# A two-layer trunk on one core: the second input unit's first chunk in float32, and the order of the head around it

## The chip, the cores and the metric

One core of one Trainium2 chip runs the whole kernel as one program. The metric is the device time of one execution, in microseconds (us), median of three runs. Its engines are TensorE (PE, with its weight loads, PEld), VectorE (DVE), ScalarE (ACT), GpSimd (POOL) and the queue of SyncE (SP), which issues nearly all DMAs.

## The reference

```python
def reference(x, norm_g, ...):
    for i in range(DEPTH):                 # DEPTH = 2: layer A, then layer B
        h = rmsnorm(x, norm_g[i])          # x * rsqrt(mean(x*x) + eps) * g
        if i % N_MIXERS == 0:
            x = x + recurrent_mixer(h, a_w_in, a_conv_w, ..., a_w_out)
        else:
            x = x + shortconv_mixer(h, b_w_in, b_conv_w, b_w_out)
    return rmsnorm(x, final_g)

def recurrent_mixer(h, w_in, conv_w, conv_b, gate_w, gate_b, lam, w_out):
    u = einsum('bsd,dc->bsc', h, w_in)     # 1024 -> 3072 columns
    gate, xb = u[..., :WIDTH], u[..., WIDTH:]
    xb = causal_depthwise_conv(xb, conv_w, conv_b)
    y = rg_lru(xb, gate_w, gate_b, lam)    # per head: two products, tanh/exp/sqrt, a scan
    return einsum('bsc,cd->bsd', y * silu(gate), w_out)
```

x is (1, 2048, 1024) in float32, WIDTH is 1536 in 12 heads of 128.

## The kernel before

The sequence is cut into 4 chunks of 512 columns; chunks 0 and 1 are half 0, chunks 2 and 3 are half 1. The 1024 inputs of a product are 8 blocks of 128 (`d`, or `kh` and `k`). A unit is 256 output columns of an input matrix: two heads' values (unit 0: `xb`) or two heads' gates (unit 1), so that layer A has 12 units. Float32 accuracy comes from three float16 products: every operand is split into a high and a low half, and `mm3` (lines 487 to 492) issues high x high, high x low and low x high, each 128x512, for one block.

Before a product of this kind, each block of x needs its norm (`normed`, L285, VectorE: x times gain times `inv`), its high half (`add`, L291, ScalarE) and its low half (L293, VectorE). The weights are scaled by a power of two found from their squares (`unit_squares` L363, `unit_scale` L372 to L381) and split (`split`, L399 on ScalarE, L401 on VectorE). `inv`, one value per column of x, is made from sums of squares by `inv_from`: a square root on ScalarE (L245), a reciprocal (L246) and four small diagonals (L256) on VectorE, four products of TensorE that spread the values over the partitions (`pn`, L259), and a copy out of PSUM (L262). For chunk 0 the squares are summed from x as it comes (L226, L227, and products `ss`, L233); for chunks 1 to 3 from rows of x, `xn`, on ScalarE (`sum_rows`, L1429).

Layer A's first two units go through `unit_of_blocks`, 16 `mm3` for a chunk, two PSUM accumulators at a time out of six (`acc_tile`). Only unit 0's chunk 0 is done otherwise: `first_weights` multiplies the weights by the norm's gain (L434, 16 pieces of 128x128), `first_blocks` takes the product with x as it comes, in float32 (L613, 16 products of 128x512), and `first_done` multiplies by `inv` afterwards (L625). The order on TensorE is: unit 0 chunk 0 in float32; unit 1 chunks 0 and 1; unit 0 chunk 1; units 1 and 0 on chunks 2 and 3; then units 2 and on. Between these products stand the `pn` of each chunk and, from the generator `mixer`, two float32 gate products for each of the two heads and each chunk (L907). `second` is a generator that is advanced twice at every stopping point of a unit; it makes the norms and blocks of chunks 1, 2 and 3. A planner orders each engine's instructions from the order of the program, priorities (`high_priority`), and extra edges (`after(a, b)`: a stands behind b); each engine then runs its instructions in that order.

Of the kernel before, what the change touches and what calls it, by code (L numbers as in the profile page):

```python
# [14 lines left out]
P = 128  # L15
# [31 lines left out]
def trunk(ctx, tc, xT, xn, prm, wa, ga, oa, wb, ob, out):  # L47
# [192 lines left out]

    def inv_from(ss, inv, queue, copy, behind=None):

        n = inv.shape[1] // P
        r = cst.tile([P, 4], F32, tag="r", name="r", bufs=2)[:, 0:n]
        s.activation(r, ss, AF.Sqrt, bias=epst[:, 0:1], scale=1.0 / D)  # L245
# [49 lines left out]
    def build_blocks(l, x, inv, ops):  # L295

        ins = []
        for c in range(2):  # L300
            for kh in range(2):
                for k in range(4):
                    n = normed(l, x[k + 4 * kh, c], k + 4 * kh, inv[c])
                    if len(ins) > 1:
                        after(n, ins[-2][1])
                    ins.append(add(ops, f"B{kh + 1}{c + 1}", k, x[k + 4 * kh, c]))
                yield ins[-1]
# [89 lines left out]
    def split(src, sw, behind=()):  # L397
        t = pair16(wp, "wc", "wc", 8)
        ins = [s.activation(t[:, 0, :], src, AF.Copy, scale=sw[:, 2:3])]  # L399
        ins.append(  # L400
            v.scalar_tensor_tensor(  # L401
                out=t[:, 1, :], in0=src, scalar=sw[:, 2:3], in1=t[:, 0, :],
                op0=ALU.mult, op1=ALU.subtract,
            )
        )
        for i, first in zip(ins, behind):
            after(i, first)
        return t

    def block_weights(l, wdram, w):  # L410


        raw = load_weights(wdram)
        yield
        sums = unit_squares(raw)
        yield
        sw = unit_scale(l, *sums, w["behind"])
        w["undo"] = sw[:, 3:4]
        for n in (0, 2, 1, 3):
            w[("A11", "A12", "A21", "A22")[n]] = split(raw[n], sw)  # L420
            yield

    def first_weights(wdram, w):


        raw, gained = ([sgt("w0") for n in range(4)] for i in range(2))
# [14 lines left out]
        sw = unit_scale(0, *sums, w["behind"])  # L441
# [51 lines left out]

    throttle, pe_last, blocks_last, evac_last = [None, None], [None], [None], [None]
# [81 lines left out]
    def unit_of_blocks(w, ops, dest, done, end, chunks=range(2), evict=None, pin=False):  # L576


        for c in chunks:
            accs = [acc_tile("acc") for m in range(2)]  # L580
            for kh in range(2):
                for k in range(4):
                    for m in range(2):
                        kk = slice(k * P, (k + 1) * P)
                        t, x = w[f"A{m + 1}{kh + 1}"], ops[f"B{kh + 1}{c + 1}", k]
                        blocks_last[0] = mm3(
                            accs[m], t[:, 0, kk], t[:, 1, kk], x[:, 0, :], x[:, 1, :],
                            kh + k == 0, kh + k == 4,
                        )
                        if pin:  # L590
                            pe_last[0] = blocks_last[0]
# [13 lines left out]
    def first_blocks(w, x):  # L605


        accs = w["accs"] = [acc_tile("acc") for m in range(2)]
        behind = None
        for d in range(KB):  # L610
            kk = slice((d % 4) * P, (d % 4 + 1) * P)
            for m in range(2):
                ins = nc.tensor.matmul(  # L613
                    accs[m], w["raw"][2 * m + d // 4][:, kk], x[d, 0],
# [4 lines left out]
            behind = yield ins  # L619

    def first_done(accs, inv, behind):
        t = [xct("xb") for m in range(2)]
        for m in range(2):
            after(
                v.tensor_tensor(out=t[m][:, 3 : 3 + CH], in0=accs[m], in1=inv, op=ALU.mult),  # L625
                behind,
            )
        return t
# [26 lines left out]
    def in_proj(l, units, ops, first, side):  # L655
# [170 lines left out]
    def in_A(ops, first, head, side, before_end, beside):  # L826
# [6 lines left out]
        def pair(hp):  # L833
# [5 lines left out]
            def conv(m, half, c, a, undo=None):  # L839
# [20 lines left out]
                with tc.high_priority(1000 if undo is not None else 1):  # L860
# [105 lines left out]

            units.append((wa[2 * hp], xdest, nothing, beside, xafter, conv))
            units.append((wa[2 * hp + 1], nothing, nothing, beside, nothing, silu))
# [404 lines left out]
    prep0 = first_weights(wa[0], w0)  # L1373
    gains()
    constants()
    x0, x1, xrows = {}, {}, {}

    def load_x(x, c):
        for d in range(KB):
# [11 lines left out]
    for kh in range(2):  # L1391
        next(prep0)
        for d in range(4 * kh, 4 * kh + 4):
            x0[d, 0] = load("A", d, 0, xt("xs"))
    prep = block_weights(0, wa[1], w1)
    next(prep)
# [5 lines left out]
    blocks0 = build_blocks(0, x0, inv0, hA[0])  # L1402
# [3 lines left out]
    w0["squares"] = sq[1], sq[2], sq[3], sq[7]  # L1406
    next(prep0)
    next(prep)

    firsts = first_blocks(w0, x0)  # L1410
    for d in range(5):
        mm = next(firsts)
    w0["behind"] = mm
    ss = ps.tile([P, 4], F32, tag="g", name="ss", bufs=2)
    with tc.high_priority(PR):
        mm = sums_of(acc, ss, mm)
    next(prep0)
    mm = w1["behind"] = firsts.send(mm)
    with tc.high_priority(PR):
        mm = inv_from(ss, inv0[0], None, v.tensor_copy, mm)  # L1420
    run(prep)
    firsts.send(mm)
    blocks_last[0] = next(firsts)
    split0 = [next(blocks0) for i in range(2)]

    def sum_rows(c, behind):
        for i, t in enumerate(xrows[c]):
            after(
                s.activation(t, t, AF.Square, accum_out=rows[c % 2][:, i : i + 1]), behind  # L1429
            )  # L1430

    def inv_of_rows(c, inv):
        with tc.high_priority(PR):
            inv_from(rows[c % 2], inv, None, v.tensor_copy, blocks_last[0])


    sum_rows(1, split0[0][0])

    def head():

        return first_done(w0["accs"], inv0[0], split0[-1][1])

    def second():
        inv_of_rows(1, inv0[1])
        split0.extend(blocks0)
        w0["split"] = split0[1][0], split0[3][1]
        run(prep0)
        yield
        h = build_blocks(0, x1, inv1, hA[1])
        for c in range(2):  # L1450
            sum_rows(2 + c, split0[2 + c][0])
            for _ in range(4 - 2 * c):
                yield
            inv_of_rows(2 + c, inv1[c])
            yield
            for _ in range(2):
                next(h)
                yield
# [7 lines left out]
    first = w0, (w1, prep)  # L1466
# [289 lines left out]
```

## Time and profile before

| | |
|---|---|
| median of 3 runs | 1963.3 us (1962.35 to 1965.16) |
| the profiled execution | 1963.37 us |
| its span in the profile | 1961.6 us |
| TensorE busy | 1927.5 us, 98% of the span |
| VectorE, ScalarE, GpSimd busy | 1267.1, 1101.7, 710.6 us |

The 1.8 us between span and execution lie outside the traced instructions. Times in the rows are microseconds from the span's start unless a column says ns. A float32 product appears as two MATMUL records, a float16 product as one.

### The profile page before, as it was taken

What the parts mean: (1) busy time and instruction counts of PE and PEld (TensorE: products, weight loads), DVE (VectorE), ACT (ScalarE), POOL (GpSimd) and SP (SyncE); (2) the same over time, 40 slices, a digit from 0 to 9 for tenths busy, and PEclk for the clock granted to TensorE, in tenths of its full rate; (3) what the DMA queues carried; (4) which work ended last, traced back from release to release, by engine and by line L of the source; (5) the groups of instructions that cost most, each with busy time, mean ns of one, the idle gap of its engine ahead of it and who ended that gap; (6) DMA issues with size and microseconds to landing.
All of it is one profiled execution on the core that took longest, in us unless ns stands there. A gap on an engine that the chain in (4) does not pass through costs nothing.

```text
span 1961.6 us, 25479 instructions
## 1 busy us (share of the span) xinstructions
PE 1927.5 (98%) x8922; PEld 900.1 (46%) x8922; DVE 1267.1 (65%) x2103; ACT 1101.7 (56%) x1970; POOL 710.6 (36%) x554
## 2 busy tenths in 40 slices
PE   7899999999999999999999999999999999999998
PEld 3344444444444444444444444444444444444446
DVE  7878667777777687999435437547547436544565
ACT  6959877777767663455454553553553543544442
POOL 0012313343413030335453454564664643622321
PEclk9999999999999999999999999999999999999999
DMA  9223323332315985411041131242232220496572
GB/s 339 71 76 107 124 71 107 103 124 86 108 43 206 377 329 168 159 61 43 33 156 54 61 128 59 77 154 70 91 129 65 81 97 28 148 368 230 111 228 87
DMA packets 158289, 252.97 MB, mean 129 GB/s; under 512 B 15312, under 2 KB 58960, under 8 KB 158160
## 3 DMA queue, kind: packets, MB, share of 16 engines
q1 hardware_dynamic: 157936, 250.82, 38.2%
q8 instruction: 70, 1.15, 0.2%
q0 software_dynamic: 224, 0.53, 0.1%
q14 instruction: 59, 0.48, 0.1%
HBM read 173.16 MB, written 78.12 MB: 128 GB/s over the span
## 4 chain that ended last, share of the span: by engine, by line
PE 81%; DVE 7%; ACT 5%; issue 4%; DMA 3%; POOL 1%; SPq 0%; DVEq 0%; POOLq 0%; ACTq 0%
PE acc L488 12%; PE acc L491 12%; PE acc L492 12%; PE p L492 8%; PE p L488 8%; PE p L491 8%; PE r L488 4%; PE r L492 4%; PE r L491 4%; PE pg L907 2%; PE q L492 2%; PE q L491 2%; PE q L488 2%; DMA xs<-in_xT 1%; DVE op L293 1%
## 5 line engine op out<-in xcount | busy, mean ns | idle before, releaser
L488 PEld LDWEIGHTS <-wc 128*128 128x128 f16 x2096 | 208.0, 99 | 266.0 <-issue 30.8
L491 PEld LDWEIGHTS <-wc 128*128 128x128 f16 x2096 | 205.7, 98 | 258.4 <-issue 24.6
L492 PEld LDWEIGHTS <-wc 128*128 128x128 f16 x2096 | 205.6, 98 | 256.6 <-issue 13.5
L488 PE MATMUL acc<-op,wc 128*128 128x512 f16 x752 | 281.2, 382 | 12.5 <-ACT op L291 11.3
L492 PE MATMUL p<-op,wc 128*128 128x512 f16 x768 | 291.1, 379 | 1.1 <-DVE wc L401 1.1
L491 PE MATMUL p<-op,wc 128*128 128x512 f16 x768 | 291.1, 379 | 0.0
L488 PE MATMUL p<-op,wc 128*128 128x512 f16 x768 | 290.6, 379 | 0.1
L491 PE MATMUL acc<-op,wc 128*128 128x512 f16 x752 | 286.9, 383 | 0.7 <-DVE op L293 0.3
L492 PE MATMUL acc<-op,wc 128*128 128x512 f16 x752 | 286.5, 382 | 0.0
L932 POOL TENSOR_TENSOR u<-fixed,u 128x512 f32<-128x512 f32 x48 | 51.3, 1091 | 366.4 <-ACT fixed L929 344.8
L227 POOL TENSOR_TENSOR sa<-sa,sq 128x512 f32<-128x512 f32 x48 | 71.5, 1490 | 270.3 <-ACT sq L226 254.4
L401 DVE SCALAR_TENSOR_TENSOR wc<-wr,fixed,wc 128x512 f16<-128x512 f32 x122 | 115.0, 960 | 78.2 <-ACT wc L399 68.6
L1312 DVE SCALAR_TENSOR_TENSOR xo<-acc,fixed,xo 128x512 f32<-128x512 f32 (+1 forms) x120 | 84.8, 710 | 104.3 <-PE acc L492 100.3
L401 DVE SCALAR_TENSOR_TENSOR wc<-ws,fixed,wc 128x512 f16<-128x512 f32 x104 | 100.1, 970 | 76.6 <-ACT wc L399 76.6
L492 PE MATMUL r<-op,wc 128*128 128x512 f16 x384 | 145.5, 379 | 0.0
L491 PE MATMUL r<-op,wc 128*128 128x512 f16 x384 | 145.5, 379 | 0.0
L488 PE MATMUL r<-op,wc 128*128 128x512 f16 x384 | 145.5, 379 | 0.0
L998 POOL TENSOR_TENSOR pb<-pb,cg 128x512 f32<-128x512 f32 x48 | 67.7, 1410 | 196.0 <-DVE fixed L375 117.3
L399 ACT ACTIVATE wc<-wr,fixed 128x512 f16<-128x512 f32 x122 | 83.8, 712 | 75.5 <-DVE fixed L378 72.6
L865 DVE SCALAR_TENSOR_TENSOR u<-acc,fixed,u 128x511 f32<-128x511 f32 (+2 forms) x138 | 101.1, 741 | 31.2 <-ACT u L861 31.0
L933 DVE TENSOR_TENSOR_SCAN u<-a,fixed,u 128x512 f32<-128x512 f32 x48 | 80.5, 1681 | 38.8 <-POOL u L932 38.8
L527 ACT ACTIVATE ed<-p,fixed 128x512 f32<-128x512 f32 x72 | 49.3, 685 | 91.1 <-PE p L492 86.0
(205 smaller groups left out, 3937.4 us busy)
## 6 DMA issues: line engine op xcount, KB each, us to landing
wr<-in_wb SPq DMA_DIRECT2D x104, 256.0 KB, 3.3
zAT<-u SPq DMA_DIRECT2D x48, 256.0 KB, 2.0
zr<-zAT SPq DMA_DIRECT2D x48, 256.0 KB, 5.2
zr<-zBT SPq DMA_DIRECT2D x48, 256.0 KB, 5.2
wr<-in_wa SPq DMA_DIRECT2D x44, 256.0 KB, 3.8
zAB<-sg SPq DMA_DIRECT2D x36, 256.0 KB, 2.1
zr<-zAB SPq DMA_DIRECT2D x36, 256.0 KB, 5.4
zBB<-ed SPq DMA_DIRECT2D x36, 256.0 KB, 2.0
```

What stands on the lines that cost most here:

```text
L227: squared[0] = eng.tensor_tensor(out=acc, in0=acc, in1=sq, op=ALU.add)
L399: ins = [s.activation(t[:, 0, :], src, AF.Copy, scale=sw[:, 2:3])]
L401: v.scalar_tensor_tensor(out=t[:, 1, :], in0=src, scalar=sw[:, 2:3], in1=t[:, 0, :], op0=ALU.mult, op1=ALU.subtract,)
L488: ins = nc.tensor.matmul(acc, wh, xh, start=start, stop=False, **kw)
L491: nc.tensor.matmul(acc, wh, xl, start=False, stop=False, **kw)
L492: return nc.tensor.matmul(acc, wl, xh, start=False, stop=stop, **kw)
L527: marked["ACT"] = s.activation(d[m, c], acc, AF.Copy, scale=undo)
L865: v.scalar_tensor_tensor(out=u[:, n:], in0=a[:, 0 : CH - n], scalar=ac(3 - n), in1=u[:, n:], op0=ALU.mult, op1=ALU.add,)
L932: marked["POOL"] = g.tensor_tensor(out=u, in0=w, in1=u, op=ALU.mult)
L933: v.tensor_tensor_scan(out=u, data0=a, data1=u, initial=stA[:, h : h + 1], op0=ALU.mult, op1=ALU.add,)
L998: g.tensor_tensor(out=t, in0=t, in1=cg[m, half, c], op=ALU.mult)
L1312: ins = v.scalar_tensor_tensor(out=x[:, ts], in0=acc[:, ts], scalar=zsc[half][:, 2:3], in1=x[:, ts], op0=ALU.mult, op1=ALU.add,)
```

## The change

Unit 1's chunk 0 is taken in float32 from x as it comes too, in the way of unit 0's. Its four weight tiles are loaded between the first blocks of x, its gained copies made by 16 more pieces of L434, and its 16 products alternate with unit 0's. The norm of chunk 0 is made behind step 7 of these 16 steps and that of chunk 1 behind step 9 (each step is two products). `first_done` now takes four accumulators out, the second pair scaled by `unscale` as well, behind the last block of chunk 1; the gate function of chunk 0 then works from these copies (`gdest`). Only three of chunk 0's eight blocks are made early; the other five come behind chunk 3's. `constants` comes behind these three. Both units' weights are split behind the square root of chunk 1's norm. The copies of `inv` for chunks 1 to 3 move from VectorE to ScalarE. The convolution of unit 0's chunk 1 loses its high priority, and `norm_last` puts a chunk's first float16 product behind the `pn` of a norm.

```diff
-def first_blocks(w, x):
-    accs = w["accs"] = [acc_tile("acc") for m in range(2)]
+def first_blocks(ws, x):
+    for w in ws:
+        w["accs"] = [acc_tile("acc") for m in range(2)]
     behind = None
-    for d in range(KB):
+    for u, d in [(u, d) for u in range(2) for d in range(2)] + [
+        (u, d) for d in range(2, KB) for u in range(2)
+    ]:
+        w = ws[u]
...
-            behind = yield ins
+            behind = (yield ins) or ins
...
 def start_blocks(w0, w1):
-    take(1, 0, w1, iter(()), True, end=nothing)
-    for m in range(2):
-        units[0][1](m, 0, 0)
+    take(1, 0, w1, iter(()), True, (1,), end=nothing)
+    for u in range(2):
+        for m in range(2):
+            units[u][1](m, 0, 0)
     take(0, 0, w0, iter(()), True, (1,))
...
-                with tc.high_priority(1000 if undo is not None else 1):
+                with tc.high_priority(1 if (hp, half, c) < (0, 0, 2) else 1000):
...
+next(prep0); gains(); load_x(x0, 0, (0, 1)); next(prep1); load_x(x0, 0, (2, 3))
+next(prep0); next(prep1); load_x(x0, 0, range(4, KB))
...
+for step in range(2 * KB):
+    mm = firsts.send(mm)
+    if step == 5:
+        w0["behind"] = w1["behind"] = mm
+        ss = ps.tile([P, 4], F32, tag="g", name="ss", bufs=2)
+        with tc.high_priority(PR):
+            mm = sums_of(acc, ss, mm)
+        next(prep1)
+        next(prep0)
+    elif step == 7:
+        with tc.high_priority(PR):
+            mm = inv_from(ss, inv0[0], None, v.tensor_copy, mm)
+        sum_rows(1, rooted * 4)
+    elif step == 9:
+        mm = inv_of_rows(1, inv0[1], mm)
+        w0["split"] = w1["split"] = rooted[0]
+        run(prep1)
+        run(prep0)
+    else:
+        mm = None
+blocks_last[0] = norm_last[0] = mm
+blocks0 = build_blocks(0, x0, 0, inv0[0], hA[0])
+for _ in range(3):
+    next(blocks0)
+constants()
+chunk1 = list(build_blocks(0, x0, 1, inv0[1], hA[0]))
+sum_rows(2, [hi for hi, _ in chunk1[0::2]])
 
 def head():
-    return first_done(w0["accs"], inv0[0], split0[-1][1])
+    return first_done((w0, w1), inv0[0], chunk1[-1][1])
 
 def second():
...
+    h = [build_blocks(0, x1, c, inv1[c], hA[1]) for c in range(2)]
+    norm_last[0] = inv_of_rows(2, inv1[0], blocks_last[0])
+    yield
+    chunk2 = list(h[0])
+    sum_rows(3, [hi for hi, _ in chunk2[0::2]])
+    for _ in range(7):
         yield
+    norm_last[0] = inv_of_rows(3, inv1[1], blocks_last[0])
+    yield
+    run(h[1])
+    yield
+    run(blocks0)
+    yield
```

## Rows read from the trace of the kernel before

**Rows 1.** The page: TensorE's busy tenths in 40 slices of 49 us.

```profile
PE   7899999999999999999999999999999999999998
```

**Rows 2.** Busy time of each engine in stretches: the stretch, its length, busy us (instructions) of PE, PEld, DVE, ACT and POOL, granted clock, share of DMA engines, GB/s.

```profile
0.00:7.00 7.00, 1.01 (x4) 0.93 (x4) 2.98 (x28) 2.15 (x8) 0.31 (x5) 1.00 0.66 182
7.00:26.00 19.00, 18.67 (x52) 9.27 (x53) 14.88 (x63) 13.68 (x30) 0.00 (x0) 1.00 1.03 385
26.00:45.00 19.00, 13.62 (x57) 6.12 (x57) 15.00 (x28) 14.78 (x26) 0.00 (x0) 0.91 1.00 354
45.00:70.00 25.00, 24.31 (x112) 11.74 (x112) 20.46 (x42) 20.53 (x36) 0.00 (x0) 0.93 0.57 193
70.00:90.00 20.00, 17.17 (x60) 7.08 (x60) 19.53 (x39) 19.81 (x33) 0.00 (x0) 1.00 0.00 0
90.00:108.00 18.00, 13.51 (x50) 5.39 (x49) 12.14 (x25) 12.86 (x19) 4.25 (x4) 0.81 0.08 30
108.00:128.00 20.00, 20.00 (x94) 9.06 (x93) 19.80 (x33) 8.72 (x18) 6.67 (x5) 1.00 0.28 92
128.00:1952.00 1824.00, 1817.52 (x8488) 849.16 (x8486) 1159.27 (x1845) 1008.47 (x1803) 697.99 (x539) 1.00 0.38 126
```

**Rows 3.** What TensorE waited for from 7 to 128 us: us in total, times, the longest.

```profile
PE acc L488 <- ACT op L291: 11.3, 6, 3.5
PE pg L907 <- DVE u L874: 1.5, 2, 1.3
```

**Rows 4.** The columns of rows 2 in stretches of 2 us, around the places where the granted clock falls.

```profile
28.00:30.00 2.00, 1.76 (x6) 0.69 (x6) 1.97 (x5) 1.21 (x3) 0.00 (x0) 0.77 1.03 370
30.00:32.00 2.00, 2.00 (x7) 0.63 (x5) 2.00 (x5) 1.37 (x3) 0.00 (x0) 0.50 0.96 339
32.00:34.00 2.00, 2.00 (x10) 0.90 (x9) 1.24 (x2) 2.00 (x5) 0.00 (x0) 0.87 0.89 238
...
46.00:48.00 2.00, 2.00 (x6) 0.71 (x5) 2.00 (x4) 0.93 (x2) 0.00 (x0) 0.54 0.98 371
48.00:50.00 2.00, 2.00 (x7) 0.80 (x6) 2.00 (x4) 2.00 (x4) 0.00 (x0) 0.61 0.37 152
...
94.00:96.00 2.00, 0.97 (x3) 0.25 (x2) 2.00 (x5) 2.00 (x5) 0.00 (x0) 0.50 0.00 0
96.00:98.00 2.00, 2.00 (x6) 0.73 (x5) 2.00 (x4) 0.81 (x2) 0.00 (x0) 0.50 0.00 0
98.00:100.00 2.00, 2.00 (x6) 0.63 (x5) 2.00 (x6) 0.80 (x3) 0.00 (x0) 0.50 0.35 131
100.00:102.00 2.00, 2.00 (x9) 0.89 (x8) 2.00 (x6) 0.09 (x1) 0.00 (x0) 0.81 0.00 0
```

**Rows 5.** TensorE in order of time: start, us, line, output and inputs, number of records [idle before, and what ended it]. The row at 59.38 is the 23rd product after the one at 54.41.

```profile
7.06 11.29 PE L613 MATMUL acc<-xs,w 128*128 128x512 f32 x20 [1.45 <-DVE fixed L171]
...
22.13 3.60 PE L613 MATMUL acc<-xs,w 128*128 128x512 f32 x8
28.11 0.59 PE L488 MATMUL acc<-op,wc 128*128 128x512 f16 x2 [2.38 <-ACT op L291]
...
44.96 1.02 PE L488 MATMUL acc<-op,wc 128*128 128x512 f16 x4 [2.33 <-ACT op L291]
...
54.41 0.38 PE L491 MATMUL acc<-op,wc 128*128 128x512 f16 x1
...
59.38 0.38 PE L488 MATMUL acc<-op,wc 128*128 128x512 f16 x1
...
70.75 0.59 PE L488 MATMUL acc<-op,wc 128*128 128x512 f16 x2 [1.44 <-ACT op L291]
...
93.61 0.72 PE L488 MATMUL acc<-op,wc 128*128 128x512 f16 x2 [3.46 <-ACT op L291]
95.36 1.44 PE L488 MATMUL acc<-op,wc 128*128 128x512 f16 x3 [1.03 <-ACT op L291]
```

**Rows 6.** Groups of instructions from 7 to 128 us: line, engine, output and inputs, shapes, count | busy us, mean ns of one | idle before.

```profile
L285 DVE SCALAR_TENSOR_TENSOR xs<-xs,fixed,inv 128x512 f32<-128x512 f32 x32 | 23.6, 744 | 0.1
L293 DVE TENSOR_TENSOR op<-xs,op 128x512 f16<-128x512 f32 x32 | 21.8, 682 | 4.4 <-ACT op L291 4.4
L1429 ACT ACTIVATE xn<-xn 128x1024 f32<-128x1024 f32 x12 | 12.5, 1041 | 0.0
L613 PEld LDWEIGHTS acc<-xs,w 128*128 128x128 f32 x32 | 6.8, 221 | 9.3 <-issue 7.3 <-DVE fixed L171 1.5 <-DMA wr<-in_wa 0.2
L262 DVE COPY inv<-pn 128x512 f32<-128x512 f32 x4 | 2.7, 684 | 1.1 <-PE pn L259 1.1
```

**Rows 7.** VectorE and ScalarE in order of time, columns as in rows 5.

```profile
10.75 0.87 DVE L434 TENSOR_SCALAR w<-w,fixed 128x128 f32<-128x128 f32 x4
13.91 0.63 ACT L226 ACTIVATE sq<-xs 128x512 f32<-128x512 f32 x1 [0.17 <-DVE sa L227]
19.68 0.87 DVE L256 TENSOR_SCALAR dg<-fixed,r 128x128 f32<-128x128 f32 x4
23.27 2.74 DVE L401 SCALAR_TENSOR_TENSOR wc<-wr,fixed,wc 128x512 f16<-128x512 f32 x4 [0.67 <-ACT wc L399]
60.25 1.28 DVE L625 TENSOR_TENSOR xb<-acc,inv 128x512 f32<-128x512 f32 x2
```

**Rows 8.** SyncE's queue: the issue of the rows of chunk 1, columns as in rows 5.

```profile
11.63 2.33 SPq L1389 DMA_DIRECT2D xn<-in_xn  x4
```

More of the change, by code (lines that the diff above doesn't have):

```diff
@@ L293, in add, with build_blocks @@
         return hi, v.tensor_tensor(out=t[:, 1, :], in0=src, in1=t[:, 0, :], op=ALU.subtract)
[L295 to L307, printed above, removed]
+    built = []
+    def build_blocks(l, x, c, inv, ops):
+        for d in range(KB):
+            n = normed(l, x[d, c], d, inv)
+            if len(built) > 1:
+                after(n, built[-2][1])
+            built.append(add(ops, f"B{d // 4 + 1}{c + 1}", d % 4, x[d, c]))
+            yield built[-1]
     def build_h(l, x, inv, ks, ops, ready=()):
@@ L395, in load_weights, with split, first_weights @@
         return raw
-    def split(src, sw, behind=()):
+    def split(src, sw, behind=None):
         t = pair16(wp, "wc", "wc", 8)
[L399 to L404, printed above, removed]
-        )
-        for i, first in zip(ins, behind):
-            after(i, first)
-        return t
[L410 to L426, printed above, removed]
+        ins = s.activation(t[:, 0, :], src, AF.Copy, scale=sw[:, 2:3])
+        if behind is not None:
+            after(ins, behind)
+        v.scalar_tensor_tensor(
+            out=t[:, 1, :], in0=src, scalar=sw[:, 2:3], in1=t[:, 0, :],
+            op0=ALU.mult, op1=ALU.subtract,
+        )
+        return t
+    def first_weights(wdram, w, raw, gained):
         w["raw"] = gained
@@ L618, in first_blocks, with first_done @@
                     after(ins, behind)
-            behind = yield ins
-    def first_done(accs, inv, behind):
-        t = [xct("xb") for m in range(2)]
+            behind = (yield ins) or ins
+    def first_done(ws, inv, behind):
+        t = [xct("xb") for n in range(4)]
+        unscale = ws[1]["scale"][:, 0:1]
+        two_over(unscale, ws[1]["undo"])
+        v.tensor_scalar(
+            out=unscale, in0=unscale, scalar1=0.5, scalar2=None, op0=ALU.mult
+        )
         for m in range(2):
-            after(
-                v.tensor_tensor(out=t[m][:, 3 : 3 + CH], in0=accs[m], in1=inv, op=ALU.mult),
-                behind,
-            )
+            ins = v.tensor_tensor(
+                out=t[m][:, 3 : 3 + CH], in0=ws[0]["accs"][m], in1=inv, op=ALU.mult
+            )
+            after(ins, behind)
+        for m in range(2):
+            ins = v.scalar_tensor_tensor(
+                out=t[2 + m][:, 3 : 3 + CH], in0=ws[1]["accs"][m], scalar=unscale,
+                in1=inv, op0=ALU.mult, op1=ALU.mult,
+            )
+            after(ins, behind)
         return t
@@ L965, in silu, with gdest @@
                 gate(m, half, c)
+            def gdest(m, half, c):
+                silu(m, half, c, heads0[2 + m][:, 3 : 3 + CH], first[1][0]["undo"])
             units.append((wa[2 * hp], xdest, nothing, beside, xafter, conv))
-            units.append((wa[2 * hp + 1], nothing, nothing, beside, nothing, silu))
+            units.append((wa[2 * hp + 1], gdest, nothing, beside, nothing, silu))
         for hp in range(NH // 2):
@@ L1372, in trunk, with load_x @@
     inv0, inv1 = [[xt("inv") for c in range(2)] for half in range(2)]
-    prep0 = first_weights(wa[0], w0)
-    gains()
-    constants()
+    prep0 = first_weights(wa[0], w0, *([sgt("w0") for n in range(4)] for i in range(2)))
+    prep1 = first_weights(
+        wa[1], w1, [wrt("wr") for n in range(4)], [buf(wk, "mx", "w1", 10) for n in range(4)]
+    )
     x0, x1, xrows = {}, {}, {}
-    def load_x(x, c):
-        for d in range(KB):
+    def load_x(x, c, blocks=range(KB)):
+        for d in blocks:
             x[d, c % 2] = load("A", d, c, xt("xs"))
@@ L1389, in load_rows @@
             sp.dma_start(t, xn[r0 : r0 + P, :])
[L1391 to L1396, printed above, removed]
+    next(prep0)
+    gains()
+    load_x(x0, 0, (0, 1))
+    next(prep1)
+    load_x(x0, 0, (2, 3))
+    next(prep0)
+    next(prep1)
+    load_x(x0, 0, range(4, KB))
     load_rows(1)
@@ L1401, in trunk @@
         load_x(x1, c)
-    blocks0 = build_blocks(0, x0, inv0, hA[0])
     acc = et("sa")
     sq = [add_square(acc, x0[d, 0], d == 0, v) for d in range(KB)]
-    w0["squares"] = sq[1], sq[2], sq[3], sq[7]
+    w0["squares"] = sq[1], sq[1], sq[3], sq[3]
+    w1["squares"] = sq[1], sq[3], sq[7], sq[7]
     next(prep0)
[L1408 to L1424, printed above, removed]
+    next(prep1)
     def sum_rows(c, behind):
         for i, t in enumerate(xrows[c]):
-            after(
-                s.activation(t, t, AF.Square, accum_out=rows[c % 2][:, i : i + 1]), behind
-            )
@@ L1432, in inv_of_rows @@
-    def inv_of_rows(c, inv):
+            ins = s.activation(t, t, AF.Square, accum_out=rows[c % 2][:, i : i + 1])
+            after(ins, behind[i])
+    def inv_of_rows(c, inv, behind):
         with tc.high_priority(PR):
-            inv_from(rows[c % 2], inv, None, v.tensor_copy, blocks_last[0])
-    sum_rows(1, split0[0][0])
+            return inv_from(rows[c % 2], inv, None, s.copy, behind)
+    firsts = first_blocks((w0, w1), x0)
+    mm = None
[6 more added lines that the diff above has]
+                mm = sums_of(acc, ss, mm)
+            next(prep1)
+            next(prep0)
+        elif step == 7:
[8 more added lines that the diff above has]
+        else:
+            mm = None
@@ L1464, in ahead @@
         return w, prep
-    first = w0, (w1, prep)
+    first = w0, (w1, iter(()))
     sideA = [second()]
```

24 lines of the change are left out of this document (7 added, 17 removed).

## The prediction, made before the changed kernel ran

> **What bounds the kernel now.** I read the page's 40 slices first [rows 1]: TensorE is at nine tenths or more nearly everywhere; the first slices fall short. The stretches [rows 2] put a size on it. From 108 us on TensorE is full (20.00 of 20, then 1817.52 of 1824), so that a microsecond which the head gives back to TensorE shifts the rest of the kernel by one. From 7 to 108 us it is not full. The waits [rows 3] say why: 11.3 us in six waits for ScalarE's high halves of blocks of x, and 1.5 us of gate products behind the convolution. Then the clock: after the three longest of these waits (2.38, 2.33, 3.46 us, the last followed by 1.03) [rows 5] the granted clock falls to its lower level, 1.2 GHz, and the float16 products take twice as long [rows 4]. Busy time by (1 - clock) over these rows is 1.66 us at 28 to 34, 1.70 at 46 to 50 and 2.87 at 94 to 102: 6.2 us. So the head loses 11.3 + 1.5 + 6.2 = 19.0 us to late operands, and this is the most that a change of the head's order can earn.
>
> The operands are late because VectorE and ScalarE are nearly full themselves: 40.0 of 45 us and 40.3 of 45 from 45 to 90 [rows 2]. A block costs VectorE 0.74 + 0.68 less some overlap, about 1.36 us [rows 6], while TensorE uses one up in six products, 1.3 us: (59.38 - 54.41)/23 = 0.216 us each [rows 5].
>
> **What the change costs.** One chunk of unit 1 (16 x 3 x 0.216 = 10.4 us of float16) becomes 16 float32 products. Eight records, four products, took 3.60 us less the last one's drain, 0.43 a record [rows 5], so 0.86 a product and 13.7 us: **3.3 us more work on TensorE**. The `ss`, `pt` and `pn` products stay the same in number: nothing.
>
> Here one rule speaks against the change. The float32 weight loads take 0.22 us on average [rows 6], and the records still follow at 0.43, so the loads lie under the products before them. The Trainium skill, "TensorE: Matmul & The Clock Gate", section "Weight-path perf modes", says that fast weight load is off for float32. Were the 32 added loads bare, they would cost 32 x 0.22 = 7.0 us more; the trace shows them covered, and I add nothing.
>
> **What it removes.** Before, float16 work began at 28.11 behind a wait of 2.38 us, because chunk 0's blocks need the norm, the copy and the splits first, all after `ss`. Now TensorE has its own work meanwhile. Its float32 phase: start at 7.06, 32 products of 0.86 = 27.5; the slow beginning, where 20 records took 11.29 us instead of 8.6, so 2.7 lost, paid in both kernels; `ss`, `pt` and `pn`, which fill 18.35 to 22.13 beside two products, 2.1; one more `pn`, about 1 [rows 5]. It ends near 40. In that time VectorE and ScalarE must finish this, in order:
>
> - Chunk 0's squares. Four weight tiles (1.05 MB) now go ahead of x's last four blocks in SyncE's queue; at 385 GB/s [rows 2] these land 2.7 us later, the last square starts at 16.6 instead of 13.91 [rows 7], the sum is ready near 18. `ss` stands behind step 5, near 20: covered by 2 us.
> - The gains: 16 pieces, 0.87 for four [rows 7], 3.5 us on VectorE before 15, where it is idle 4.1 of 19 us [rows 2]; half a microsecond of wait at worst.
> - Chunk 1's norm: rows asked for at 11.63 as before, since the bytes ahead are the same [rows 8]; four squares of 1.04 + 0.1 on ScalarE [rows 6] behind a square root near 21, another root, the reciprocal and 0.87 us of diagonals [rows 7]: ready near 27. Its `pn` stands behind step 9, near 29. All later float32 products are queued behind it on TensorE; the cover is 2 us, and beyond that each microsecond costs one.
> - Splits of eight weight tiles, 2.74 us for four on VectorE [rows 7], 5.5 in all, three blocks of chunk 0, 4.1, then chunk 1's. From 25.5 on this gives the first block of chunk 1 near 37 to 38.5, with TensorE there at 40. The cover is thin; if `constants` or the gains spill over it is gone. I keep half of what the same place costs now, (2.38 + 1.66)/2 = **2.0 us**.
>
> Chunk 1's eight blocks then run ahead of TensorE, and so do chunk 2's: unit 1 chunk 1 and unit 0 chunk 1 fill TensorE from 40 to about 62, while VectorE owes 8 + 8 blocks, four copies out of PSUM (0.64 each [rows 7]), and two gate functions: 22 + 2.6 + 2.6 = 27 us from 35. So the waits at 44.96 and 70 go, with the first's slow stretch. Five blocks of chunk 0 (5 x 1.36 = 6.8 us) are no longer in their way.
>
> Chunk 3 is where it is late next. Its norm is only asked for at the middle of unit 1's chunk 2, near 67, and the blocks compete with two convolutions. Before, that place cost 3.46 + 1.03 idle and 2.87 of clock, 7.4 us. With 6.8 us less ahead of them but TensorE here some 10 us earlier, I take half, **3.7 us**. The small waits between gate products stay as they are, 1.5 and the short ones, **1.9 us** in all. The copies of three `inv` go from VectorE (0.68 each [rows 6]) to ScalarE, and are taken at nothing: ScalarE's share from 90 to 128 is 21.6 of 38 [rows 2], and if that cover fails they cost 0.7 each. The five late blocks are needed only by unit 2, after 108, and cost nothing while TensorE has units 0 and 1's half 1 to do; without it, 6.8 us.
>
> The clock is the second rule that I weigh. The rows show that stalls of 2.3 us and more are followed by a stretch at 0.50, and one of 1.44 at 70 is not: the clock stays at 1.00 behind it [rows 2, 5]. The Trainium skill, same page, section "What's actually happening", calls the half rate the default that activity lifts. By it each long stall avoided earns its slow stretch too, which is what the sum already does.
>
> **Sum.** 19.0 recoverable, less 3.3, less what stays (2.0 + 3.7 + 1.9 = 7.6): 8.1 us gained. The profiled execution took 1963.4 us, its span 1961.6 and 1.8 around it; it stands 0.1 above the median. 1963.3 - 8.1 = **1955.2 us**.
>
> **The rivals.**
>
> 1. *Nearly all waits go.* If chunk 3 is covered too (TensorE can take unit 0's chunk 2 meanwhile, as the planner may order it), only 2 to 3 us stay: 19.0 - 3.3 - 2.5 = 13.2, 1950. For it: the other unit's products are there to fill in. Against: VectorE. Chance 0.14.
> 2. *VectorE becomes the bound of the head.* Its busy time up to 128 us is 104.8 [rows 2]; gains 3.5 and two more copies 1.3 come, 2.0 of `inv` copies go: 107.6. At its share of 45 to 90 us, 40.0/45 = 0.89, the work after 7 us lasts (107.6 - 3.0)/0.89 = 117.5 us, to 124.5 instead of 128: 3.5 us gained, 1959.8. Against: scans and gate functions can wait, TensorE doesn't need them by then. Chance 0.18.
> 3. *The second norm is late on TensorE.* 4 us late at `pn`, with a slow stretch of 1.7, would leave 2.4: 1960.9. Chance 0.06.
> 4. *Bare weight loads*, as worked out: 8.1 - 7.0 = 1.1 gained, 1962.2. Chance 0.02.
> 5. *Slower: the accumulators.* Four of six are now held from the first products until chunk 1's last block, and unit 1's chunk 1 takes the other two. Unit 0's chunk 1 cannot start before two are copied out. If VectorE takes chunk 2's eight blocks (10.9 us) ahead of these copies, TensorE stands about 11 us near 51, and starts again at 0.50 for the 2.9 us that such a stall cost before. 14 us on top of the 7.6: 19.0 - 3.3 - 21.6 = -5.9, 1969. It decides from a wait of about 5 us, with its clock. For it: the blocks come first in the program. Against: chunk 2's norm needs squares behind chunk 1's blocks, then two engines and `pn`, which leaves VectorE some 3 us free just then. Chance 0.12.
>
> **The numbers.** The forecast itself has 0.48, with 1951.5 to 1958.5 of its own (the terms that stay between 4 and 11 us). About 0.2%, 4 us, is what a measurement here tells from no change. Faster by more: the forecast, rival 1 and half of rival 2, with a little of 3: 0.72. Within: the rest of 2, 3 and 4: 0.16. Slower: rival 5, 0.12. The low end is the ceiling with nothing left of the waits, 1963.3 - 15.7 = 1947.6, rounded to 1947; the high end takes in rivals 2 to 4 and leaves the slower case out: 1963.
>
> **What would show it.** Right: 64 records of L613, ending near 40, with no gap over a microsecond; the float16 stream beginning within 2 us of it; granted clock 1.00 from 28 to 70; one falling stretch at most, at chunk 3's start. Wrong: TensorE waiting for `pn` near 29; a wait of several microseconds near 51 for a copy by VectorE (L625's successor); a wait for L291 and half clock at two places again; or VectorE at 19 of 20 from 45 on with TensorE below it. The prediction is wrong also if TensorE after 128 us is no longer full.

## The result, and the profile after

The changed kernel takes 1952.2 us (median of 4 runs, 1950.99 to 1953.28) against 1964.2 of the kernel before in the same comparison (1962.35 to 1966.74): a ratio of 0.9938, 95% interval 0.9926 to 0.9949, so 12.0 us faster. The profiled execution took 1953.3 us, its span 1951.5, which is 10.1 us less than the profiled execution before.

The stretches of the changed kernel (columns as in [rows 2]):

```profile
7.00:26.00 19.00, 17.61 (x49) 8.53 (x49) 16.12 (x87) 14.49 (x33) 0.00 (x0) 1.00 1.02 372
26.00:41.00 15.00, 15.00 (x47) 7.47 (x46) 14.89 (x32) 8.95 (x17) 0.00 (x0) 1.00 1.01 353
41.00:62.00 21.00, 14.51 (x57) 6.93 (x56) 18.73 (x36) 13.79 (x26) 0.00 (x0) 0.76 0.65 249
62.00:73.00 11.00, 11.00 (x52) 5.00 (x51) 9.08 (x18) 10.94 (x19) 0.00 (x0) 1.00 0.32 96
73.00:90.00 17.00, 17.00 (x80) 8.27 (x79) 15.44 (x32) 12.98 (x25) 0.00 (x0) 1.00 0.06 17
90.00:108.00 18.00, 18.00 (x76) 8.20 (x74) 15.25 (x25) 15.94 (x24) 2.13 (x2) 1.00 0.03 11
108.00:128.00 20.00, 20.00 (x90) 9.23 (x89) 15.63 (x35) 14.00 (x26) 3.59 (x3) 1.00 0.34 109
```

TensorE is full from 26 to 41 us and from 62 us on. One stretch, 41 to 62, holds nearly the whole loss. What it waited for from 7 to 128 us, where [rows 3] had six waits for ScalarE:

```profile
PE pn L261 <- DVE dg L258: 6.5, 1, 6.5
PE ss L233 <- DVE sa L227: 0.9, 1, 0.9
PE acc L605 <- DVE fixed L114: 0.5, 1, 0.5
```

The six waits for high halves are gone, and so are the gate products' waits. In their place is one wait of 6.5 us. TensorE in order of time (columns as in [rows 5]; L605 are the float32 products, L261 the products that spread a norm):

```profile
7.71 12.20 PE L605 MATMUL acc<-xs,w 128*128 128x512 f32 x24 [0.49 <-DVE fixed L114]
20.82 1.05 PE L233 MATMUL ss<-fixed,sa 128*128 128x1 f32 x8 [0.90 <-DVE sa L227]
...
30.02 1.05 PE L261 MATMUL pn<-dg,fixed 128*128 128x128 f32 x8
30.91 10.46 PE L605 MATMUL acc<-xs,w 128*128 128x512 f32 x24
...
53.05 2.07 PE L261 MATMUL pn<-dg,fixed 128*128 128x128 f32 x8 [6.49 <-DVE dg L258]
77.57 1.05 PE L261 MATMUL pn<-dg,fixed 128*128 128x128 f32 x8
```

The float32 phase runs through to 41.4 and float16 work follows without a gap. At 46.6, in the middle of unit 1's chunk 1, stand the four products of chunk 2's norm, and everything behind them waits until 53.05. They themselves then run at half speed: eight records in 2.07 us, where the same eight at 77.57 take 1.05. What they wait for, on VectorE and ScalarE:

```profile
41.54 1.06 ACT L1424 ACTIVATE xn<-xn 128x1024 f32<-128x1024 f32 x1 [2.03 <-DMA xn<-in_xn]
47.70 1.04 ACT L1424 ACTIVATE xn<-xn 128x1024 f32<-128x1024 f32 x1
49.26 0.28 ACT L247 ACTIVATE r<-fixed 128x4 f32<-128x4 f32 x1
50.00 1.28 DVE L622 TENSOR_TENSOR xb<-acc,inv 128x512 f32<-128x512 f32 x2
51.20 0.17 DVE L248 RECIPROCAL r<-r 128x4 f32<-128x4 f32 x1
51.28 1.38 DVE L627 SCALAR_TENSOR_TENSOR xb<-acc,fixed,inv 128x512 f32<-128x512 f32 x2
52.71 0.87 DVE L258 TENSOR_SCALAR dg<-fixed,r 128x128 f32<-128x128 f32 x4
```

The rows of chunk 2 land late, their squares are tied to chunk 1's blocks on ScalarE, the last begins at 47.7, and the diagonals (L258) stand behind the four copies out of PSUM on VectorE.

One more reading tells the head from what comes behind it. A small product for a weight scale (`pt`) stands behind the same work in both kernels: 32 float32 and 408 float16 records before, 64 and 360 here, and 24 records of gate products in both. It is called the mark below. Its start before (L372) and here (L374):

```profile
148.93 0.28 PE L372 MATMUL pt<-fixed 128*128 128x4 f32 x2
140.79 0.28 PE L374 MATMUL pt<-fixed 128*128 128x4 f32 x2
```

TensorE is 8.1 us ahead there. The other 2.0 of the 10.1 us come later.

### The profile page after: what moved, and what is told of

Same layout as the page of the kernel before. It is cut to its first block, busy times and chain, and to the rows that moved or that the text cites. A ratio compares the mean times of both kernels' runs of the same rounds, so it can differ in the third digit from the quotient of the medians.

```text
span 1951.5 us, 25464 instructions
## 1 busy us (share of the span) xinstructions
PE 1926.0 (99%) x8906; PEld 901.2 (46%) x8906; DVE 1267.5 (65%) x2120; ACT 1101.9 (56%) x1971; POOL 708.2 (36%) x554
## 4 chain that ended last, share of the span: by engine, by line
PE 89%; DVE 5%; DMA 3%; ACT 2%; issue 1%; POOL 0%; SPq 0%; DVEq 0%; ACTq 0%; POOLq 0%
PE acc L475 14%; PE acc L478 14%; PE acc L479 14%; PE p L479 8%; PE p L478 8%; PE p L475 8%; PE r L475 4%; PE r L479 4%; PE r L478 4%; PE pg L912 3%; PE q L479 2%; PE q L478 2%; PE q L475 2%; DVE op L295 1%; DMA xs<-in_xT 1%
## 5 line engine op out<-in xcount | busy, mean ns | idle before, releaser
L479 PE MATMUL acc<-op,wc 128*128 128x512 f16 x736 | 279.7, 380 | 0.0
L478 PE MATMUL acc<-op,wc 128*128 128x512 f16 x736 | 279.7, 380 | 0.0
L475 PE MATMUL acc<-op,wc 128*128 128x512 f16 x736 | 278.3, 380 | 0.6 <-DVE sg L966 0.3
```

Of the source, the lines that this page charges most:

```text
L475: ins = nc.tensor.matmul(acc, wh, xh, start=start, stop=False, **kw)
L478: nc.tensor.matmul(acc, wh, xl, start=False, stop=False, **kw)
L479: return nc.tensor.matmul(acc, wl, xh, start=False, stop=stop, **kw)
```

## The experiments

Two things are to be told apart. First, what earned the gain: the second float32 chunk as cover (theory F, that of the prediction) or the order of norms and blocks (theory O). Second, whether the 6.5 us left are a matter of the place in TensorE's queue (theory Q) or of what the other engines can deliver (theory V). One caution for all of them: the planner lays out the whole kernel anew for every edit, and the last pair below shows how far that alone can move the time.

**The order without float32.**

```diff
+    sum_rows(1, rooted[0])
     firsts.send(mm)
     blocks_last[0] = next(firsts)
+    inv_of_rows(1, inv0[1])
...
-            inv_from(rows[c % 2], inv, None, v.tensor_copy, blocks_last[0])
+            inv_from(rows[c % 2], inv, None, s.copy, blocks_last[0])
...
-                with tc.high_priority(1000 if undo is not None else 1):
+                with tc.high_priority(1 if (hp, half, c) < (0, 0, 2) else 1000):
```

> The kernel before, unit 1's chunk 0 in float16 as before, with the part of the new order that does not need float32: chunk 1's squares behind the first square root and its norm right behind the float32 products, copies of the later norms on ScalarE, the convolution of unit 0's chunk 1 without its priority. Theory F (the second float32 chunk covers the wait for chunk 0's blocks, and that is most of the gain): TensorE still waits before its first float16 product and at chunk 1 or 3, and the time is within 4 us of 1964. Theory O (the order of norms and blocks is the gain): 1952 to 1956.

Measured: 1954.9 us (ratio 0.9958, 0.9945 to 0.9971), 8.7 us faster than before without a single added float32 product. Theory F said within 4 us of 1964; it fails, and theory O holds for most of the gain. TensorE does still wait ahead of its float16 products, as F says (2.2 us for chunk 1's norm, 1.2 for a block, with the clock at 0.77 from 26 to 41), but at the mark, 141.58, it is 7.35 us ahead of the kernel before. Its longest wait, 4.0 us ahead of 121.8, is for a convolution. The 2.7 us between this kernel and the changed one are in the direction of F, but smaller than what a new layout can do.

**The two halves of that order, one at a time.** The convolution's priority alone:

> The kernel before with one edit: the convolution of unit 0's chunk 1 loses its high priority. The order without the second float32 chunk gave 8.7 us. If the priority is what carries it (blocks go ahead of the convolution on VectorE, so that the wait at chunk 3's start, 4.5 us and 2.9 us of slow clock, goes): 1955 to 1958. If the earlier norm of chunk 1 carries it: 1962 to 1964.5.

Measured: 1964.4 us against 1964.4, ratio 1.0001 (0.9992 to 1.0010). Nothing; the wait of 3.46 us at chunk 3's start is there as before. The earlier norm alone (the first two added lines above):

> The kernel before with chunk 1's squares behind the first square root and its norm right behind the float32 products, copies on VectorE and the convolution's priority as before. If the earlier norm carries the gain of the order (the wait of 2.3 us at chunk 1's start goes with its slow stretch of 1.7, and VectorE is some 10 us ahead afterwards): 1955 to 1958. If the priority carries it: 1960 to 1964, the 4 us at chunk 1 at best.

Measured: 1957.0 us, ratio 0.9956 (0.9944 to 0.9969). The earlier norm of chunk 1 carries 7.4 us by itself; at the mark, 142.35, it is 6.6 us ahead. The edit makes both the squares and the norm's products on TensorE earlier, and the two were not taken apart; the third part of that order, the copies of `inv` on ScalarE, was not run by itself. Why it helps is seen on ScalarE and VectorE. In the kernel before:

```profile
22.51 2.56 ACT L399 ACTIVATE wc<-wr,fixed 128x512 f16<-128x512 f32 x4 [3.08 <-DVE fixed L378]
31.28 1.04 ACT L1429 ACTIVATE xn<-xn 128x1024 f32<-128x1024 f32 x1
34.39 1.04 ACT L1429 ACTIVATE xn<-xn 128x1024 f32<-128x1024 f32 x1
36.08 0.69 DVE L293 TENSOR_TENSOR op<-xs,op 128x512 f16<-128x512 f32 x1 [2.84 <-ACT op L291]
```

and with the earlier norm, in the same view:

```profile
20.84 1.05 ACT L1415 ACTIVATE xn<-xn 128x1024 f32<-128x1024 f32 x1
26.41 1.04 ACT L1415 ACTIVATE xn<-xn 128x1024 f32<-128x1024 f32 x1
```

The stretch from 26 to 41 us in the kernel before, then two stretches with the earlier norm (columns as in [rows 2]):

```profile
26.00:41.00 15.00, 11.95 (x47) 5.10 (x47) 11.84 (x23) 10.80 (x20) 0.00 (x0) 0.89 1.01 356
26.00:41.00 15.00, 10.71 (x46) 4.94 (x46) 14.33 (x27) 7.77 (x14) 0.00 (x0) 0.89 1.05 391
90.00:108.00 18.00, 17.45 (x82) 7.88 (x81) 17.56 (x24) 13.10 (x21) 6.28 (x4) 1.00 0.08 30
```

Before, ScalarE stood idle 3.08 us ahead of 22.5, and then put the four squares, from 31.3 on, in front of high halves that VectorE waited 2.84 us for. With the earlier norm the squares begin at 20.8, in that idle time, and VectorE is busy 14.33 of 15 us from 26 to 41 instead of 11.84, and 17.56 of 18 from 90 to 108 instead of 12.14 [rows 2 for the latter]. The large wait at chunk 3 is gone with it: TensorE is busy 17.45 of 18 there, where it was 13.51. Smaller waits take its place elsewhere (0.5 to 2.2 us, for norms and for blocks): from 8 to 128 us TensorE still stands 11.8 us, after 13.7. The larger part of the gain is the clock: by (1 - clock), summed over stretches of 2 us, slow stretches cost 2.9 us there instead of 6.2.

**Float32 without the order.**

```diff
-            mm = inv_of_rows(1, inv0[1], mm)
+            mm = None
...
-    for _ in range(3):
-        next(blocks0)
+    all0 = list(blocks0)
+    sum_rows(1, [all0[3][0]] * 4)
     constants()
+    inv_of_rows(1, inv0[1], blocks_last[0])
     chunk1 = list(build_blocks(0, x0, 1, inv0[1], hA[0]))
-    sum_rows(2, [hi for hi, _ in chunk1[0::2]])
+    sum_rows(2, [chunk1[3][0]] * 4)
...
-                with tc.high_priority(1 if (hp, half, c) < (0, 0, 2) else 1000):
+                with tc.high_priority(1000 if undo is not None else 1):
```

(Against the changed kernel; its early squares of chunk 1 go too.)

> The changed kernel with unit 1's chunk 0 in float32, but chunk 1's norm made behind the fourth block of chunk 0 and spread behind the float32 products, all eight blocks of chunk 0 ahead of chunk 1's, and the convolution's priority as before the change. Theory F (the float32 chunk is cover enough by itself): 1954 to 1959. Theory O (the wait only moves from chunk 0's blocks to chunk 1's, which stand behind the same 11 us of VectorE): TensorE waits 5 us or more near 41 with a slow stretch, 1959 to 1966.

Measured: 1966.3 us, ratio 1.0008 (0.9999 to 1.0017): no gain, and 0.3 above the range of theory O. Its waits from 7 to 128 us:

```profile
PE pn L261 <- DVE dg L258: 8.7, 3, 3.4
PE acc L475 <- ACT op L293: 2.1, 1, 2.1
PE ss L233 <- DVE sa L227: 1.3, 1, 1.3
PE acc L605 <- DVE fixed L114: 0.6, 1, 0.6
```

Three norms wait in TensorE's queue, one for each of chunks 1 to 3 (3.4, 3.05 and 2.2 us), and chunk 1's first block behind the first of them. The float32 products push the wait from chunk 0's blocks to chunk 1's norm and first block and pay 3.3 us for it, as theory O said. At the mark TensorE is 1.7 us ahead; a wait of 3.0 us for a gate function ahead of 206 us and 3.3 us of slow clock behind it take that back. Chunk 2's norm stands where the changed kernel has it, so that this is not quite the kernel before with float32 alone.

| kernel | TensorE at the mark | ahead of the kernel before |
|---|---|---|
| before | 148.93 us | |
| earlier norm of chunk 1 alone | 142.35 us | 6.6 us |
| order without float32 | 141.58 us | 7.35 us |
| float32 without the order | 147.25 us | 1.7 us |
| the change | 140.79 us | 8.1 us |

By the mark, ahead of which the float32 and float16 work is the same but for the exchanged chunk, the order is worth 7.35 of the 8.1 us. The 0.8 that the float32 chunk adds to it is not told from nothing: each is one profiled execution, and the first float32 product alone begins between 6.4 and 7.7 us in them.

**Parts of the order, undone in the changed kernel.** All eight blocks of chunk 0 first (`range(8)` for `range(3)`):

> The changed kernel, with all eight blocks of chunk 0 made ahead of chunk 1's instead of three. That puts five blocks, 6.8 us of VectorE, ahead of chunk 1's first. If making them later is a needed part of the gain: TensorE waits some 4 to 7 us for chunk 1's first block near 41, with a slow stretch behind, and the time is 1957 to 1963. If VectorE has that much to spare there: within 2 us of 1952; and since the wait at chunk 2's norm comes after chunk 1's blocks it would move later as well.

Measured: 1957.0 us, ratio 0.9970 (0.9959 to 0.9981), 4.8 us slower than the changed kernel (4.5 at the mark). TensorE waits 3.2 us for chunk 1's first block at 45.4, at 0.50 behind it, and still 5.5 us for chunk 2's norm. Chunk 1's norm behind step 15 instead of 9:

> The changed kernel, with chunk 1's norm spread behind the last float32 product instead of behind step 9. If its place between the products is a needed part: chunk 1's first block comes 10 us later, TensorE waits 3 us or more near 41, and the time is 1956 to 1964. If the blocks of chunk 1 are not the bound: within 2 us of 1952.

Measured: 1955.5 us, ratio 0.9960 (0.9946 to 0.9974), 3.3 us slower (3.8 at the mark). TensorE waits 2.2 us at 43.9, with no slow stretch behind it, and 6.7 for chunk 2's norm. Each step is thus visible as a wait of the kind and nearly the place expected; at the second, wait and time are smaller than the least that I gave (3 us and 1956).

**The 6.5 us that stay.** Chunk 2's norm spread at the end of unit 1's chunk 1:

```diff
+        for _ in range(2):
+            yield
         norm_last[0] = inv_of_rows(2, inv1[0], blocks_last[0])
...
-        for _ in range(7):
+        for _ in range(5):
             yield
```

> The changed kernel with one edit: the four products that spread chunk 2's norm stand behind the end of unit 1's chunk 1 on TensorE, not behind its middle. In the changed kernel they wait 6.5 us there for their diagonals, with everything behind them, and 2.9 us of half clock follow. Theory Q (they are early in the queue, the work behind them is ready): the wait falls to under 2 us, the half clock goes, and the time falls by 5 to 9 us below the changed kernel, to 1943 to 1947 us. Theory V (VectorE is the bound there: chunk 1's last blocks, or the accumulators, would stop TensorE at the same place): the wait only changes its name, and the time stays within 2 us of the changed kernel's 1952.

Measured: 1961.8 us, ratio 0.9989 (0.9980 to 0.9998): slower than the changed kernel by 9.6 us. Neither theory had that. TensorE:

```profile
52.23 1.16 PE L261 MATMUL pn<-dg,fixed 128*128 128x128 f32 x8 [0.35 <-DVE dg L258]
75.84 0.80 PE L261 MATMUL pn<-dg,fixed 128*128 128x128 f32 x2 [6.91 <-DVE dg L258]
```

The wait at chunk 2's norm does go (0.35), as Q says. TensorE comes to chunk 3's norm that much earlier and waits 6.9 us there, with half clock behind. So far that is even; the rest is lost further back, in waits that the changed kernel has not: 3.0 us for a gate function on VectorE at 202.7, with 1.6 us of slow clock behind it, and 0.9 and 1.0 before. The second attempt leaves the norm's place and makes its input earlier, chunk 2's rows loaded ahead of its blocks and squared earlier:

> The changed kernel with the norm of chunk 2 left where it stands in TensorE's queue, and what it waits for made earlier: its four rows of x are loaded ahead of chunk 2's blocks in SyncE's queue, and squared behind the first four blocks of chunk 1 on ScalarE instead of behind every second one. If the rows and their squares are what the 6.5 us wait is for: it falls under 2 us, and the kernel is no slower than 1953; where the 9 us go then is seen at chunk 3's norm, which waited 6.9 us when TensorE came early to it, so 1947 to 1957. If VectorE's order (the diagonals behind the copies out of PSUM) is what it is for: the wait stays over 4 us.

Measured: 1960.2 us, ratio 0.9980 (0.9971 to 0.9989). The wait at chunk 2's norm falls from 6.5 to 1.15 us, so that the rows and squares were its cause; chunk 3's norm then waits 6.5. The same picture by another way, a wait of 3.0 us at 201.8 included, and the time missed the range that I gave. The third alternates the units on chunks 2 and 3, so that chunk 3's norm has ten microseconds more, and moves chunk 2's norm as above (the part on `second` is left out here):

```diff
-            take(1, 1, w1, none, True)
-            take(0, 1, w0, prep, True)
+            take(1, 1, w1, none, True, (0,), end=nothing)
+            take(0, 1, w0, none, True, (0,), end=nothing)
+            take(1, 1, w1, none, True, (1,))
+            take(0, 1, w0, prep, True, (1,))
...
```

> The changed kernel with the order on TensorE changed in two places: chunk 2's norm spread behind the end of unit 1's chunk 1, and units 1 and 0 alternating on chunks 2 and 3 (1, 0 on chunk 2, then 1, 0 on chunk 3), with chunk 3's norm spread behind the middle of unit 0's chunk 2. When chunk 2's norm alone was moved, the wait moved to chunk 3's norm (6.9 us) and the kernel was slower by 9.6 us. Theory Q (norms that are early in TensorE's queue, and nothing else): neither norm waits over 2 us, and the time is 1944 to 1949. Theory V (VectorE's work of the head is the bound; what TensorE gains before 108 us it gives back behind it, waiting for accumulators): the two waits go, TensorE waits elsewhere after 108 us, and the time is 1951 to 1962.

Measured: 1951.7 us, ratio 0.9934 (0.9921 to 0.9946): the same as the changed kernel. Both norms' waits are gone (0.6 in all), and TensorE waits 2.0 us for unit 2's weight splits near 114, then 1.2, 1.7 and 1.7 us elsewhere. The fourth mends the splits, which that edit had made late:

> The kernel of the alternating order once more, with the splits of unit 2's weights advanced from unit 0's chunk 2 on, as in the order before, where the first version left them to unit 0's chunk 3 and TensorE waited 2.0 us for them near 114 with 1.7 us of slow clock behind. If that was all that kept it at 1951.7: 1946 to 1949. If VectorE is the bound there, the wait changes its name and it stays at 1950 to 1953.

Measured: 1956.9 us, ratio 0.9965 (0.9952 to 0.9977): slower, though its head is the best of all. TensorE's busy time to 200 us:

```profile
41.00:62.00 21.00, 21.00 (x101) 9.96 (x100) 20.43 (x38) 15.89 (x29) 0.00 (x0) 1.00 0.71 264
108.00:128.00 20.00, 20.00 (x85) 8.91 (x84) 20.00 (x37) 18.84 (x32) 2.13 (x2) 1.00 0.28 93
128.00:160.00 32.00, 32.00 (x133) 14.51 (x132) 26.05 (x52) 28.63 (x46) 10.85 (x8) 1.00 0.37 115
160.00:200.00 40.00, 34.56 (x130) 14.74 (x129) 31.84 (x61) 37.36 (x68) 9.98 (x8) 0.91 0.25 86
```

From 41 to 160 us TensorE is full at full clock, and at the mark, 131.44, it is 9.4 us ahead of the changed kernel. Then it stands 5.4 us between 160 and 200, at 0.91 of the clock: a gate product waits 3.0 us for a convolution on VectorE, a float16 product 2.4 us for a tanh on ScalarE. It stands 3.7 us more where layer B's first weights are split. The order on TensorE is not the reason in the first stretch: from the mark to the next product of its kind, as many float16 records stand between any two gate products as in the changed kernel. Two gate products in a row and the end of the convolution that the second needs, in the changed kernel (L912, L874) and here (L914, L876):

```profile
171.18 1.02 PE L912 MATMUL pg<-u,gts 128*128 128x512 f32 x2
174.36 0.20 DVE L874 TENSOR_SCALAR fixed<-acc,fixed 128x3 f32<-128x3 f32 x1
175.93 1.02 PE L912 MATMUL pg<-u,gts 128*128 128x512 f32 x2
161.83 1.02 PE L914 MATMUL pg<-u,gts 128*128 128x512 f32 x2
169.52 0.20 DVE L876 TENSOR_SCALAR fixed<-acc,fixed 128x3 f32<-128x3 f32 x1
169.77 2.08 PE L914 MATMUL pg<-u,gts 128*128 128x512 f32 x2 [3.04 <-DVE fixed L876]
```

TensorE comes 9.35 us earlier, VectorE's convolution only 4.8. By the next product of the mark's kind (195.71 against 196.55) 0.8 us of the lead is left. What the head gained was given back behind it, as theory V says, to engines that are not that much earlier.

**Is it ScalarE's load?** ScalarE is at 37.36 of 40 us there. The last pair leaves out part of the computation that falls into this stretch, from the kernel just shown and, as a control, from the changed kernel (the scale of layer A's output weights is a constant, without its loads and squares).

> The alternating order with unit 2's splits in time (TensorE without a wait from 8 to 160 us, then 3.0 and 2.4 us of waits between 160 and 200, with ScalarE at 37.4 of 40 us there), with part of the computation left out: the 24 loads and squares of layer A's output weights that give their scale (0.72 us each on ScalarE, 17 us in all, from about 165 us on; the scale is a constant instead). Theory V, for ScalarE: these waits are what the head's gain is given back to; they shrink to under 2 us together, with the slow stretch of 3.6 us, and the time falls from 1957 to 1949 to 1952. If ScalarE is not what TensorE waits for there: 1955 to 1958, the waits in place.

Measured: 1955.8 us (1951.9 to 1957.3), ratio 0.9950 (0.9938 to 0.9963). ScalarE falls to 33.63 of 40 us, and TensorE still stands 6.1 of 40 us there, 2.8 and 2.2 of it for the tanh. But the order on TensorE is no longer the same: between the fourth and the fifth gate product behind the mark stand 16 float16 records instead of 10.

> The changed kernel with the same part of the computation left out. There TensorE has 0.2 us of waits between 160 and 200 us, so by theory V, with nothing given back there, the time stays within 2 us of 1952, and it is the control for the run above. If it falls as well by 5 us or more, the squares cost every kernel something that the waits don't show.

Measured: 1958.3 us, ratio 0.9967 (0.9955 to 0.9979), 6.1 us **slower** than the changed kernel, with work taken out. At the mark, 140.70, it is level with it; behind, TensorE's gate products wait 4.5 us for the tanh between 160 and 200 us, where the changed kernel waits 0.2. Here too 16 float16 records stand where the changed kernel has 10. So these squares on ScalarE are not what TensorE waits for, and theory V falls for ScalarE's load. Two causes are left for waits in that stretch: TensorE comes earlier than the other engines (the kernel of the alternating order, in an unchanged order), or the planner puts the gate products in another place (the control, without a lead). For the second it is argued, not shown: no run moves the gate products alone.

## Why the prediction was right, and where its reasons were not

- *The time.* 1955.2 was forecast, 1952.2 measured; faster by 8.1 and by 12.0. The likeliest case was the one that came, near its better end. At the mark TensorE is ahead by just the 8.1 forecast; the sum that gave it was not right, as shown below.
- *The float32 phase.* End near 40, measured 41.4. 24 records in 10.46 us are 0.43 each, so 3.3 us more work and covered weight loads (0.20 us on average, 64 of them) are right, and rival 4 is out. The Trainium skill ("TensorE: Matmul & The Clock Gate", section "Weight-path perf modes") says that fast weight load is off for float32; the trace agrees in so far as such a load takes 0.20 us where one in float16 takes 0.10. It just doesn't show in the spacing.
- *The cover in it.* `ss` was to be covered by 2 us and waited 0.9; the gains half a microsecond at worst, measured 0.5; chunk 1's norm on time at 30.02, so rival 3 did not come at that place. The first float16 product: 2.0 us kept, nothing measured.
- *Chunk 3 and the small waits.* 3.7 and 1.9 us kept, nothing measured. VectorE had the slack (15.4 of 17 and 15.3 of 18 us from 73 to 108), so rival 2 is out.
- *The step that failed* is "So the waits at 44.96 and 70 go". I weighed the norm of chunk 1 as a product that holds up TensorE's queue, and not that of chunk 2, which stands in the middle of unit 1's chunk 1 and is named only in rival 5, as a reason why VectorE would be free. It waited 6.5 us, and the clock behind it cost, by (1 - clock) as in the prediction, 2.9. Rival 5 had the place and nearly the size (11 us near 51, for copies by VectorE), and not the mechanism: the accumulators were free in time (with that norm moved behind unit 1's chunk 1, TensorE is busy 20.65 of 21 us from 41 to 62), and the copies only stood ahead of the norm's diagonals for 2.7 us of it. The sign "granted clock 1.00 from 28 to 70" failed with it: the clock stood at 0.50 from 53 to 58.
- *The sum.* What stays was 7.6 and is 6.5 + 2.9 + 0.9 = 10.3. By that the head gains 19.0 - 3.3 - 10.3 = 5.4 us, not 8.1. At the mark it gains 8.1 all the same, so 2.7 us come from places that the sum left out. The slow beginning cost 1.7 instead of 2.5 (24 records in 12.20 us against 10.3, 20 in 11.29 against 8.6, both less a drain of 0.2), though it began 0.65 later; the rest was not traced. That the head comes out as forecast is luck: two errors of 2.7 us offset each other. The 2.0 us behind the mark go with TensorE's idle time in the middle of the kernel: from 128 to 1900 us it was 5.3 us before (100.00 - 98.57 from 200 to 300, 700.00 - 696.12 from 300 to 1000), and it is 3.0 here (1812.00 - 1809.01, with nothing added up to 1940). The forecast had nothing for it.

```profile
128.00:1940.00 1812.00, 1809.01 (x8442) 844.48 (x8441) 1156.85 (x1842) 1006.96 (x1794) 700.78 (x543) 1.00 0.38 126
```

- *The reason.* I put the gain down to TensorE having float32 work of its own while the blocks are made. The runs show that this is the smaller part, if any. Float32 without the order earned 1.7 us at the mark and nothing in the end (1966.3), the earlier norm of chunk 1 without float32 7.4 us (1957.0), the order without float32 8.7 (1954.9). I had costed the move of that norm only by whether it comes in time, not by the idle time of ScalarE that its squares move into and the wait of VectorE that they leave. [Rows 2] had it: VectorE was busy 12.1 of 18 us from 90 to 108 while TensorE waited for its blocks, so it was not simply full, as I wrote, but held up.
- *That a microsecond which the head gives back shifts the rest of the kernel by one* held to within 2.0 us for this change and fails beyond it: the kernel without any wait from 41 to 160 us is 9.4 us ahead of the changed one at the mark and slower by 4.7 in the end.

## What to carry to other kernels

When an engine's operands are late, look first for who stands idle and who stands in front of whom on the engines that make them: here making one norm earlier, its four squares in an idle stretch of ScalarE, earned 7.4 us, and giving TensorE other work meanwhile, by itself, nothing. A small product that depends on a long chain holds up the queue as much as a large one (here eight records of 1.05 us held it for 6.5); check the place of each, not only of the one that is moved. An engine that comes earlier than those that feed it gives the lead back. And where a planner lays out the kernel anew at every edit, run a control whose edit lies elsewhere before a difference of some microseconds is put down to the edit: here one moved the time by 6 us.

## What the runs showed of the hardware that was not expected

- After the 6.5 us wait the clock stood at its lower level, 0.50, and the norm's eight records took 2.07 us instead of 1.05. A wait of 2.0 us near 114 us (the alternating order) was also followed by a stretch at 0.50, and the one of 1.44 us at 70 in the kernel before was not [rows 5]. The length of the wait alone does not decide it: waits of 2.2 us (at 43.9 with chunk 1's norm behind step 15, at 84.0 in float32 without the order) were followed by none, and of two waits of 3.02 us ahead of the same product, the one that ended at 202.65 (chunk 2's norm moved) was followed by a stretch at 0.50 and the one at 201.79 (its rows earlier) was not.
- ScalarE's copy of `inv` out of PSUM took 0.56 us against VectorE's 0.68, so that it is cheaper there than the 0.7 that I named for it:

```profile
32.52 0.56 ACT L264 COPY inv<-pn 128x512 f32<-128x512 f32 x1
```

- Two scans of the same shape on VectorE took 2.11 and 1.27 us, 2.6 us apart in the alternating order; GpSimd was at work until 105.70, through half of the first (two products from 102.03, 3.67 us). It is not the only pair: of the scans that stand alone in the timeline of the kernel before from 80 to 900 us, all 21 without GpSimd at work took 1.25 to 1.28 us, and 22 of the 25 with it 1.88 to 2.34. That it is the cause was not tried.

```profile
104.67 2.11 DVE L940 TENSOR_TENSOR_SCAN u<-a,fixed,u 128x512 f32<-128x512 f32 x1
107.29 1.27 DVE L940 TENSOR_TENSOR_SCAN u<-a,fixed,u 128x512 f32<-128x512 f32 x1
102.03 3.67 POOL L939 TENSOR_TENSOR u<-fixed,u 128x512 f32<-128x512 f32 x2 [101.19 <-ACT fixed L936]
```
